# Rotary embedding with cached tables: one VectorE operation for both products of a chunk, from interleaved tables

## The chip, the cores and the metric

One core of one Trainium2 chip. The metric is the device time of one execution in microseconds (us), lower is better; each kernel was run several times beside the kernel before on the same chip.

## The reference, cut to what matters

```python
def setup_inputs():
    batch, n_heads, seq, head_dim = (8, 8, 1024, 64)
    ...
    return {'x': np.random.randn(batch, n_heads, seq, head_dim).astype(np.float32), 'cos_cached': ..., 'sin_cached': ...}

def reference(x, cos_cached, sin_cached):
    half = x.shape[-1] // 2
    x_first, x_second = (x[:, :, :, :half].copy(), x[:, :, :, half:].copy())
    out_first = x_first * cos_cached - x_second * sin_cached
    out_second = x_first * sin_cached + x_second * cos_cached
    return np.concatenate([out_first, out_second], axis=-1).astype(np.float32)
```

16.8 MB of x are read and 16.8 MB written, all fp32. Per element there are two products and one sum.

## The kernel before

x is cut into 8 units of 2 MB: 128 partitions, each with 64 rows of 64 elements. A unit is loaded into its own tile, rotated in place and stored from there. Most units go in three chunks (24, 24 and 16 rows) like this: ScalarE copies ("stages") a chunk into PSUM; VectorE multiplies the staged rows by the sine table into a separate tile `s` and by the cosine table into x; and then somebody makes the sums: POOL (GpSimd), VectorE itself (the chunks called "alone"), or TensorE, which adds by multiplying with plus and minus the identity and whose result ScalarE copies back. Unit 2 is worked on by POOL from end to end.

```python
def products(pt, u, n0, n1, alone=False):
    xr, sr, pr = rows(xt[u], n0, n1), rows(s_of(u), n0, n1), rows(pt, 0, n1 - n0)
    mul(nc.vector, sr, pr, tab(sn, n0, n1))
    mul(nc.vector, pr if alone else xr, pr, tab(cs, n0, n1))
    if alone:
        sums(nc.vector, xr, pr, sr)
...
on_pool(2, 0, 32)                       # unit 2: products and sums on POOL, two halves
cuts = ((0, 24), (24, 48), (48, 64))
chunks = [(u, n0, n1) for u in (1, 3, 4, 5, 6, 7) for n0, n1 in cuts]
alone = {(1, 48), (3, 48), (6, 48), (7, 24), (7, 48)}
...
for c, (u, n0, n1) in enumerate(chunks):
    products(st[c], u, n0, n1, (u, n0) in alone)
    put(c + 2)                          # ScalarE stages the chunk after next
    if c in back:
        pe_back(*back[c])               # ScalarE copies a TensorE sum tile back into x
    if c in on_pe:
        pe_sums(*on_pe[c])
    for f, *args in behind.get(c, ()):  # POOL's sums, and the stores
        f(*args)
```

All loads of x and all stores are issued on one queue, that of the sync engine, in the order: sine table, units 0 to 7; then stores of units 0, 1, 3, 2, 4, 5, 6 and of unit 7 in two pieces, "7a" (48 rows) and "7b" (16 rows).

## Time and profile before

| | before |
|---|---|
| time, median | 85.84 us (3 runs, 85.73 to 85.88) |
| span in the profile | 83.8 us |
| VectorE busy | 72.3 us (86%) |
| POOL busy | 65.9 us (79%) |
| DMA, share of 16 engines' span | 96% |
| last store issued / landed | 77.3 / 82.7 us |

"Landed" is the issue time plus the profile's time from issue to landing. The lines themselves stand in the prediction below.

### The profile page before, as it was taken

The numbers are of one execution on the slowest core, as the hardware profiler recorded it, in microseconds if no ns is written. First come the engines' busy times: TensorE is split into PE (matmuls) and PEld (weight loads), VectorE is DVE, ScalarE is ACT, GpSimd is POOL, SyncE is SP. The second block draws the span as 40 slices with busy tenths as digits, with TensorE's granted clock in tenths as the row PEclk, the third lists the DMA queues.
The fourth block names the chain that finished last, engine by engine and source line by source line (L and its number), as shares of the span: only waits on it lengthen the run. The fifth ranks groups of instructions, "written<-read, shape, count | busy, mean of one in ns | idle before, by whom it ended". The sixth has DMA issues, their size and how long they took to land. (4 is left out here: it accounts for less than half of the span.)

```text
span 83.8 us, 409 instructions
## 1 busy us (share of the span) xinstructions
PE 42.4 (51%) x80; PEld 16.2 (19%) x80; DVE 72.3 (86%) x56; ACT 37.2 (44%) x32; POOL 65.9 (79%) x35
## 2 busy tenths in 40 slices
PE   0299910003994965949469089594959800000000
PEld 0234100002341403314033042231404200000000
DVE  1284999999999999999999999999999999998000
ACT  4100694464066553674636951976346852000000
POOL 5059959999999999999999999999999959400000
PEclk9999999999999999999999999999999999655555
DMA  2999999999999999999999999999999999999990
GB/s 59 309 411 450 415 461 391 461 415 454 415 415 454 399 469 399 446 422 415 352 415 446 415 446 407 462 415 446 422 422 454 399 450 407 462 415 434 417 385 23
DMA packets 2689, 33.83 MB, mean 404 GB/s; under 512 B 320, under 2 KB 320, under 8 KB 512
## 3 DMA queue, kind: packets, MB, share of 16 engines
q1 hardware_dynamic: 2640, 33.69, 95.7%
q10 hardware_dynamic: 48, 0.13, 0.4%
q14 instruction: 1, 0.01, 0.0%
HBM read 17.04 MB, written 16.78 MB: 404 GB/s over the span
## 5 line engine op out<-in xcount | busy, mean ns | idle before, releaser
L97 ACT COPY st<-x 128x1536 f32<-128x1536 f32 (+1 forms) x18 | 23.4, 1302 | 18.2 <-DVE x L83 10.2
L161 PE MATMUL acc<-x,ones 128*128 128x512 f32 x36 | 20.4, 650 | 20.6 <-ACT x L167 11.3
L83 DVE TENSOR_TENSOR s<-st,sn 128x1536 f32<-128x1536 f32 (+1 forms) x18 | 28.2, 1568 | 0.0
L83 DVE TENSOR_TENSOR x<-st,cs 128x1536 f32<-128x1536 f32 (+1 forms) x13 | 21.6, 1663 | 0.0
L86 POOL TENSOR_TENSOR x<-x,s 128x1024 f32<-128x1024 f32 (+3 forms) x7 | 15.8, 2262 | 1.9 <-ACT x L167 0.9
L87 POOL TENSOR_TENSOR x<-x,s 128x1024 f32<-128x1024 f32 (+3 forms) x7 | 15.8, 2258 | 0.0
L161 PEld LDWEIGHTS acc<-x,ones 128*128 128x128 f32 x36 | 6.6, 204 | 33.6 <-ACT x L167 17.9
L167 ACT COPY x<-acc 128x1024 f32<-128x1024 f32 x9 | 9.1, 1010 | 6.5 <-PE acc L162 6.5
L162 PE MATMUL acc<-s,minus 128*128 128x512 f32 x18 | 10.1, 644 | 0.0
L83 POOL TENSOR_TENSOR x<-x,cs 128x2048 f32<-128x2048 f32 x2 | 9.1, 4540 | 0.2
L162 PE MATMUL acc<-s,ones 128*128 128x512 f32 x18 | 9.2, 592 | 0.0
L83 POOL TENSOR_TENSOR g<-x,sn 128x2048 f32<-128x2048 f32 x2 | 9.1, 4532 | 0.0
L83 DVE TENSOR_TENSOR st<-st,cs 128x1024 f32<-128x1024 f32 (+1 forms) x5 | 6.6, 1328 | 0.0
L139 POOL COPY sn<-sn 32x1024 f32<-32x1024 f32 x3 | 3.1, 1032 | 3.4 <-DVE sn L136 3.3
L133 PE MATMUL en<-raw,ones 32*128 32x512 f32 x4 | 3.7, 1089 | 3.7 <-DMA raw<-in_sin_cached_dram 3.7
L86 POOL TENSOR_TENSOR x<-x,g 128x1024 f32<-128x1024 f32 x2 | 4.7, 2350 | 0.2
L97 ACT COPY pre<-x 128x2048 f32<-128x2048 f32 x1 | 1.9, 1870 | 6.6 <-DMA x<-in_x_dram 6.6
L87 POOL TENSOR_TENSOR x<-x,g 128x1024 f32<-128x1024 f32 x2 | 4.7, 2358 | 0.0
L162 PEld LDWEIGHTS acc<-s,minus 128*128 128x128 f32 x18 | 3.7, 206 | 4.9 <-issue 4.9
L162 PEld LDWEIGHTS acc<-s,ones 128*128 128x128 f32 x18 | 3.4, 190 | 4.3 <-issue 4.3
L86 DVE TENSOR_TENSOR x<-st,s 128x512 f32<-128x512 f32 (+1 forms) x5 | 3.7, 745 | 0.2
L87 DVE TENSOR_TENSOR x<-st,s 128x512 f32<-128x512 f32 (+1 forms) x5 | 3.7, 733 | 0.0
(23 smaller groups left out, 25.9 us busy)
## 6 DMA issues: line engine op xcount, KB each, us to landing
x<-in_x_dram SPq DMA_DIRECT2D x7, 2048.0 KB, 24.8
out_dram<-x SPq DMA_DIRECT2D x7, 2048.0 KB, 10.1
x<-in_x_dram SPq DMA_DIRECT2D x2, 1024.0 KB, 6.4
out_dram<-x SPq DMA_DIRECT2D x1, 1536.0 KB, 7.7
out_dram<-x SPq DMA_DIRECT2D x1, 512.0 KB, 5.4
raw<-in_cos_cached_dram ACTq DMA_DIRECT2D x1, 128.0 KB, 3.2
raw<-in_sin_cached_dram SPq DMA_DIRECT2D x1, 128.0 KB, 2.8
```

Source lines behind the costliest of these rows:

```text
L83: eng.tensor_tensor(out=o, in0=a, in1=t, op=TT.mult)
L86: eng.tensor_tensor(out=o[:, :, 0], in0=c[:, :, 0], in1=s[:, :, 1], op=TT.subtract)
L87: eng.tensor_tensor(out=o[:, :, 1], in0=c[:, :, 1], in1=s[:, :, 0], op=TT.add)
L97: nc.scalar.copy(out=pt[:, :(n1 - n0) * hd], in_=xt[u][:, n0 * hd:n1 * hd])
L133: nc.tensor.matmul(part, sel, r, start=True, stop=True)
L139: nc.gpsimd.tensor_copy(out=t[k * Q:(k + 1) * Q, C:], in_=t[0:Q, C:])
L161: nc.tensor.matmul(a[:, k], plus, xr[:, :, k], start=True, stop=False)
L162: nc.tensor.matmul(a[:, k], plus if k else minus, sr[:, :, 1 - k], start=False, stop=True)
L167: nc.scalar.copy(out=rows(xt[u], n0, n0 + G), in_=a)
```

## The change

The aim was to relieve VectorE of operations, and POOL of part of unit 2. The two tables are interleaved in one tile (32 cosines, 32 sines per row), and each unit's tile lies beside a "room" for sine products, shared with a second unit, so that one VectorE operation can write both products: its output steps from the room to the unit (a step of one whole unit, or of 40 rows for unit 7, backwards for some) and its input reads the staged rows twice. The time won pays for the products of 24 rows of unit 2, which POOL no longer makes. Two chunks lose their "alone" sums, one TensorE sum tile goes, POOL takes those sums, and the negated identity is made by ScalarE.

```diff
-    cs = const.tile([P, T], fp32, name="cs")
-    sn = const.tile([P, T], fp32, name="sn")
+    tb = const.tile([P, 2 * T], fp32, name="tb")
+    tb4 = tb.rearrange("p (n t j) -> p n t j", t=2, j=half)
 ...
+    for i, (u0, u1) in enumerate(((3, 6), (0, 4), (1, 5))):
+        w = xp.tile([P, 3 * F], fp32, name=f"w{i}")
+        xt[u0], xt[u1] = w[:, :F], w[:, 2 * F:]
+        sv[u0] = sv[u1] = w[:, F:2 * F]
+        px[u0], px[u1] = both(w[:, :2 * F]), both(w[:, F:])[:, :, ::-1]
+    K = 40
 ...
-    nc.vector.tensor_scalar_mul(out=minus, in0=plus, scalar1=-1.0)
+    nc.scalar.mul(out=minus, in_=plus, mul=-1.0)
 ...
-        mul(nc.vector, sr, pr, tab(sn, n0, n1))
-        mul(nc.vector, pr if alone else xr, pr, tab(cs, n0, n1))
+        if u not in px:                 # rows of unit 2: two operations as before
+            ...
+        xr = pt[:, :n * hd].rearrange("p (n o f) -> p n o f", o=1, f=hd)
+        tr = tb4[:, n0:n1].unsqueeze(3).to_broadcast([P, n, 2, 2, half])
+        mul(nc.vector, px[u][:, n0:n1].rearrange("p n t (k j) -> p n t k j", k=2),
+            xr.to_broadcast([P, n, 2, hd]).rearrange("p n t (k j) -> p n t k j", k=2), tr)
 ...
-    on_pool(2, 0, 32)
+    on_pool(2, 0, K // 2)
 ...
+    chunks.insert(9, (2, K, R))
-    alone = {(1, 48), (3, 48), (6, 48), (7, 24), (7, 48)}
+    whole = {(6, 48), (7, 24), (7, 48)}
 ...
-        1: [(pool_sums, 1, 32, 48), (on_pool, 2, 32, 64)],
-        3: [(store, 1)],
-        8: [(store, 3), (store, 2), (pool_sums, 4, 16, 64)],
-        9: [(store, 4)],
+        2: [(pool_sums, 1, 16, 64), (store, 1)],
+        5: [(pool_sums, 3, 32, 64), (on_pool, 2, K // 2, K)],
+        6: [(store, 3)],
+        9: [(pool_sums, 2, K, 64), (store, 2), (pool_sums, 4, 32, 64), (store, 4)],
```

More of the change, by code (lines that the diff above doesn't have):

```diff
@@ L42 @@
     xp = ctx.enter_context(tc.tile_pool(name="xp", bufs=1))
-    tv = ctx.enter_context(tc.tile_pool(name="tv", bufs=3))
-    tg = ctx.enter_context(tc.tile_pool(name="tg", bufs=1))
-    cs = const.tile([P, T], fp32, name="cs")
-    sn = const.tile([P, T], fp32, name="sn")
+    tb = const.tile([P, 2 * T], fp32, name="tb")
+    tb4 = tb.rearrange("p (n t j) -> p n t j", t=2, j=half)
     ones = const.tile([P, 2 * P], fp32, name="ones")
@@ L50, with both @@
     minus = const.tile([P, P], fp32, name="minus")
-    raw = tv.tile([P, F], fp32, name="raw", tag="s")
-    rs, rc = raw[0:Q, 0:C], raw[0:Q, C:2 * C]
+    xt, sv, px = {}, {}, {}
+    def both(t):
+        return t.rearrange("p (w n f) -> p n w f", w=2, f=hd)
+    for i, (u0, u1) in enumerate(((3, 6), (0, 4), (1, 5))):
[4 more added lines that the diff above has]
+    K = 40
+    w = xp.tile([P, K * hd + F], fp32, name="w3")
+    gt, xt[7] = w[:, :K * hd], w[:, K * hd:]
+    sv[7], px[7] = gt, both(w[:, :2 * K * hd])[:, :, ::-1]
+    xt[2], sv[2] = xp.tile([P, F], fp32, name="x2"), sv[3]
+    rs, rc = sv[3][0:Q, 0:C], sv[3][0:Q, C:2 * C]
     nc.sync.dma_start(out=rs, in_=sin_cached.rearrange("(q n) j -> q (n j)", q=Q))
     nc.scalar.dma_start(out=rc, in_=cos_cached.rearrange("(q n) j -> q (n j)", q=Q))
-    xt = [xp.tile([P, F], fp32, name=f"x{u}") for u in range(n_u)]
     for m0, m1 in ((0, F // 2), (F // 2, F)):
@@ L72 @@
                             base=0, pattern=[[-1, P]], channel_multiplier=1)
-    nc.vector.tensor_scalar_mul(out=minus, in0=plus, scalar1=-1.0)
+    nc.scalar.mul(out=minus, in_=plus, mul=-1.0)
+    cs, sn = tb4[:, :, 0], tb4[:, :, 1]
     def rows(t, n0, n1):
@@ L78, in tab, with flat @@
     def tab(t, n0, n1):
-        v = t[:, n0 * half:n1 * half].rearrange("p (n o j) -> p n o j", o=1, j=half)
-        return v.to_broadcast([P, n1 - n0, 2, half])
+        return t[:, n0:n1].unsqueeze(2).to_broadcast([P, n1 - n0, 2, half])
+    def flat(t):
+        return t.rearrange("p (n j) -> p n j", j=half)
     def mul(eng, o, a, t):
@@ L87, in sums, with products, alone @@
         eng.tensor_tensor(out=o[:, :, 1], in0=c[:, :, 1], in1=s[:, :, 0], op=TT.add)
-    sv = {}
-    def s_of(u):
-        if u not in sv:
-            sv[u] = tv.tile([P, F], fp32, name="s", tag="s")
-        return sv[u]
     def stage(pt, u, n0, n1):
         nc.scalar.copy(out=pt[:, :(n1 - n0) * hd], in_=xt[u][:, n0 * hd:n1 * hd])
-    def products(pt, u, n0, n1, alone=False):
-        xr, sr, pr = rows(xt[u], n0, n1), rows(s_of(u), n0, n1), rows(pt, 0, n1 - n0)
+    def products(pt, u, n0, n1):
+        n = n1 - n0
+        if u not in px:
+            for o, t in ((sv[u], sn), (xt[u], cs)):
+                mul(nc.vector, rows(o, n0, n1), rows(pt, 0, n), tab(t, n0, n1))
+            return
+        xr = pt[:, :n * hd].rearrange("p (n o f) -> p n o f", o=1, f=hd)
+        tr = tb4[:, n0:n1].unsqueeze(3).to_broadcast([P, n, 2, 2, half])
+        mul(nc.vector, px[u][:, n0:n1].rearrange("p n t (k j) -> p n t k j", k=2),
+            xr.to_broadcast([P, n, 2, hd]).rearrange("p n t (k j) -> p n t k j", k=2), tr)
+    def alone(pt, u, n0, n1):
+        s = sv[4] if u == 7 else sv[u]
+        xr, sr, pr = rows(xt[u], n0, n1), rows(s, n0, n1), rows(pt, 0, n1 - n0)
         mul(nc.vector, sr, pr, tab(sn, n0, n1))
-        mul(nc.vector, pr if alone else xr, pr, tab(cs, n0, n1))
-        if alone:
-            sums(nc.vector, xr, pr, sr)
+        mul(nc.vector, pr, pr, tab(cs, n0, n1))
+        sums(nc.vector, xr, pr, sr)
     def on_pool(u, n0, n1):
-        g = tg.tile([P, F // 2], fp32, name="g")
-        xr, gr = rows(xt[u], n0, n1), rows(g, 0, n1 - n0)
+        xr, gr = rows(xt[u], n0, n1), rows(gt, n0, n1)
         mul(nc.gpsimd, gr, xr, tab(sn, n0, n1))
@@ L115, in pool_sums @@
         xr = rows(xt[u], n0, n1)
-        sums(nc.gpsimd, xr, xr, rows(s_of(u), n0, n1))
+        sums(nc.gpsimd, xr, xr, rows(sv[u], n0, n1))
     def store(u, n0=0, n1=R):
@@ L135 @@
         for t, r in ((sn, rs), (cs, rc)):
-            nc.vector.stream_shuffle(t[0:Q, C:], r, odd)
-        for t in (sn, cs):
-            for k in range(1, P // Q):
-                nc.gpsimd.tensor_copy(out=t[k * Q:(k + 1) * Q, C:], in_=t[0:Q, C:])
-        mul(nc.vector, rows(s_of(0), 0, H), rows(xt[0], 0, H), tab(en, 0, H))
+            nc.vector.stream_shuffle(t[0:Q, H:], flat(r), odd)
+        for k in range(1, P // Q):
+            nc.gpsimd.tensor_copy(out=tb4[k * Q:(k + 1) * Q, H:], in_=tb4[0:Q, H:])
+        mul(nc.vector, rows(sv[0], 0, H), rows(xt[0], 0, H), tab(flat(en), 0, H))
         for i in range(2):
             xr = rows(xt[0], i * G, (i + 1) * G)
-            mul(nc.vector, xr, xr, tab(ec[i], 0, G))
+            mul(nc.vector, xr, xr, tab(flat(ec[i]), 0, G))
         pool_sums(0, 0, H)
         stage(pre, 0, H, R)
-        nc.scalar.copy(out=sn[:, :C], in_=en)
+        nc.scalar.copy(out=sn[:, :H], in_=flat(en))
         for i in range(2):
-            nc.scalar.copy(out=cs[:, i * BK:(i + 1) * BK], in_=ec[i])
+            nc.scalar.copy(out=cs[:, i * G:(i + 1) * G], in_=flat(ec[i]))
         products(pre, 0, H, R)
@@ L158, in pe_sums @@
         a = acc[u, n0].rearrange("p (k n j) -> p k n j", k=2, j=half)
-        xr, sr = rows(xt[u], n0, n0 + G), rows(s_of(u), n0, n0 + G)
+        xr, sr = rows(xt[u], n0, n0 + G), rows(sv[u], n0, n0 + G)
         for k in range(2):
@@ L167, in pe_back @@
         nc.scalar.copy(out=rows(xt[u], n0, n0 + G), in_=a)
-    on_pool(2, 0, 32)
+    on_pool(2, 0, K // 2)
     cuts = ((0, 24), (24, 48), (48, 64))
     chunks = [(u, n0, n1) for u in (1, 3, 4, 5, 6, 7) for n0, n1 in cuts]
-    alone = {(1, 48), (3, 48), (6, 48), (7, 24), (7, 48)}
-    on_pe = {0: (1, 0), 1: (1, 16), 3: (3, 0), 4: (3, 16), 6: (3, 32), 8: (4, 0),
-             9: (5, 0), 11: (5, 16), 12: (6, 0)}
-    back = {1: (1, 0), 3: (1, 16), 4: (3, 0), 6: (3, 16), 8: (3, 32), 9: (4, 0),
-            11: (5, 0), 12: (5, 16), 14: (6, 0)}
-    behind = {
-        1: [(pool_sums, 1, 32, 48), (on_pool, 2, 32, 64)],
-        3: [(store, 1)],
-        8: [(store, 3), (store, 2), (pool_sums, 4, 16, 64)],
-        9: [(store, 4)],
-        11: [(pool_sums, 5, 32, 64)],
-        12: [(store, 5)],
-        13: [(pool_sums, 6, 16, 48)],
-        14: [(store, 6)],
-        15: [(pool_sums, 7, 0, 24)],
-        16: [(store, 7, 0, 48)],
-        17: [(store, 7, 48, 64)],
+    chunks.insert(9, (2, K, R))
+    whole = {(6, 48), (7, 24), (7, 48)}
+    on_pe = {0: (1, 0), 3: (3, 0), 4: (3, 16), 6: (4, 0), 7: (4, 16), 10: (5, 0),
+             11: (5, 16), 13: (6, 0)}
+    back = {2: (1, 0), 4: (3, 0), 6: (3, 16), 8: (4, 0), 9: (4, 16), 11: (5, 0),
+            13: (5, 16), 15: (6, 0)}
+    behind = {
+        2: [(pool_sums, 1, 16, 64), (store, 1)],
+        5: [(pool_sums, 3, 32, 64), (on_pool, 2, K // 2, K)],
+        6: [(store, 3)],
+        9: [(pool_sums, 2, K, 64), (store, 2), (pool_sums, 4, 32, 64), (store, 4)],
+        12: [(pool_sums, 5, 32, 64)],
+        13: [(store, 5)],
+        14: [(pool_sums, 6, 16, 48)],
+        15: [(store, 6)],
+        16: [(pool_sums, 7, 0, 24)],
+        17: [(store, 7, 0, 48)],
+        18: [(store, 7, 48, 64)],
     }
@@ L202 @@
     for c, (u, n0, n1) in enumerate(chunks):
-        products(st[c], u, n0, n1, (u, n0) in alone)
+        (alone if (u, n0) in whole else products)(st[c], u, n0, n1)
         put(c + 2)
```

## The prediction

> **What bounds the kernel now.** I read the page's activity rows first, because one of them decides the case: which row is full in every slice.
>
> ```profile
> DVE  1284999999999999999999999999999999998000
> POOL 5059959999999999999999999999999959400000
> DMA  2999999999999999999999999999999999999990
> GB/s 59 309 411 450 415 461 391 461 415 454 415 415 454 399 469 399 446 422 415 352 415 446 415 446 407 462 415 446 422 422 454 399 450 407 462 415 434 417 385 23
> ...
> q1 hardware_dynamic: 2640, 33.69, 95.7%
> ...
> HBM read 17.04 MB, written 16.78 MB: 404 GB/s over the span
> ```
>
> VectorE and POOL are full from 10 to about 70 us, but DMA is full from the second slice to the last but one, and its one queue is busy 95.7% of the span. The view by windows says whether "full" means moving bytes at one rate, or waiting:
>
> ```profile
> 28.00:44.00 16.00, 11.45 (x27) 4.42 (x26) 15.97 (x13) 8.36 (x9) 15.84 (x7) 1.00 1.00 417
> 44.00:60.00 16.00, 11.48 (x27) 4.45 (x26) 16.00 (x12) 10.52 (x9) 15.92 (x6) 1.00 1.01 432
> 60.00:78.00 18.00, 5.56 (x13) 1.99 (x11) 17.21 (x15) 5.80 (x5) 11.27 (x6) 0.83 1.00 429
> ```
>
> The last two columns are the DMA share and GB/s: the share is 1.00 and the rate 417 to 432 in each, loads (to 44 us) and stores (after it) alike. Then the stores: first their issues in the sync queue's timeline, then, in the same order, their times to landing in the DMA view, each asked for alone (units 3 and 2, and the two last pieces of unit 7, called 7a and 7b):
>
> ```profile
> 48.53 0.33 SPq L119 DMA_DIRECT2D out_dram<-x  x1
> ...
> 51.75 0.33 SPq L119 DMA_DIRECT2D out_dram<-x  x1
> ...
> 73.79 0.33 SPq L119 DMA_DIRECT2D out_dram<-x  x1
> ...
> 77.34 0.33 SPq L119 DMA_DIRECT2D out_dram<-x  x1
> ```
>
> ```profile
> out_dram<-x SPq DMA_DIRECT2D x1, 2048.0 KB, 9.7
> ...
> out_dram<-x SPq DMA_DIRECT2D x1, 2048.0 KB, 11.4
> ...
> out_dram<-x SPq DMA_DIRECT2D x1, 1536.0 KB, 7.7
> ...
> out_dram<-x SPq DMA_DIRECT2D x1, 512.0 KB, 5.4
> ```
>
> Issue plus landing time gives when each ends. The last load (x7) is issued at 6.55 and lands 37.1 later, at 43.65; the stores in issue order (units 0, 1, 3, 2, 4, 5, 6, 7a, 7b) land at 48.6, 53.4, 58.2, 63.15, 68.0, 73.05, 77.9, 81.5 and 82.7. The steps of the 2 MB ones are 4.8 to 5.0 us, with no longer one among them: **no store ever came late.** Each was issued while the one ahead of it was still moving. The chain of waits shows VectorE (38% of the span) up to the last store's issue at 77.34, which looks as if VectorE set the end. It does not: 7b waited in the queue behind 7a until about 81. The queue sets the end, and it moves the same bytes before and after.
>
> **Slack.** In the windows, the first packets move at about 1.7 us, 1.0 after the first issue at 0.74; at the end the packets stop at about 82.2, some 0.5 before the last landing. So a store leaves no gap if it is issued by (landing of the one ahead) - 0.5 - 1.0. Latest harmless issues: unit 2 at 56.7, unit 4 at 61.65, 5 at 66.5, 6 at 71.55, 7a at 76.4, 7b at 80.0. Before, they were issued at 51.75, 58.53, 63.15, 67.78, 73.79 and 77.34: 2.6 to 5 us early.
>
> **What the Trainium skill says.** "VectorE: DVE Perf Modes", § The perf-mode tier table: fp32 tensor_tensor, and any with a PSUM operand, runs at 1x, one element a cycle; § The TRN2 errata gives an fp32 add of N elements as (N+151)/0.96 ns. The trace agrees: 1757 by that for N = 1536 against 1746 measured, 691 for 512 against 692. So merging two products halves neither reads nor time; it saves a fixed part. "SBUF — State Buffer", § Who interferes with whom: a VectorE instruction with at most one SBUF input does not contend with GpSimd. The trace fits: POOL's 1024-element sums keep 2.34 us beside a VectorE that never rests, and the merged operation again has one input in PSUM (the staged rows) and one in SBUF (the table). "DMA: Bandwidth & Descriptors", § Where 436 GB/s comes from: a ceiling of 435 GB/s on the SBUF side; the windows' 429 to 432 lie 1% below, so no change to the engines can make the transfers much quicker.
>
> **The change part by part.** Prices, from the groups by form and two rows of the timeline:
>
> ```profile
> L83 DVE TENSOR_TENSOR s<-st,sn 128x1536 f32<-128x1536 f32 x12 | 21.0, 1746 | 0.0
> L86 DVE TENSOR_TENSOR x<-st,s 128x512 f32<-128x512 f32 x4 | 2.8, 692 | 0.1
> L86 POOL TENSOR_TENSOR x<-x,s 128x1024 f32<-128x1024 f32 x4 | 9.4, 2340 | 0.9 <-POOL cs L139 0.9
> L83 POOL TENSOR_TENSOR g<-x,sn 128x2048 f32<-128x2048 f32 x2 | 9.1, 4532 | 0.0
> ```
>
> ```profile
> 16.52 1.75 DVE L83 TENSOR_TENSOR s<-st,sn 128x1536 f32<-128x1536 f32 x1
> 18.19 1.75 DVE L83 TENSOR_TENSOR x<-st,cs 128x1536 f32<-128x1536 f32 x1
> ```
>
> The starts are 1.67 apart: 1.60 for 1536 elements at 0.96 a ns, and 0.07 fixed. The sums walk all three operands in runs of 32 and still fit the same line, so I take the new patterns (runs of 64, a step to the room beside the unit and back) to cost nothing either. A merged operation on 24 rows is then 3072/0.96 = 3.20 + 0.07 = 3.27 from start to start, and on 16 rows 2.20.
>
> VectorE, by starts: 16 merged pairs (unit 0's second half, eleven of 24 rows, four of 16) save 16 x 0.07 = 1.1. Two chunks (units 1 and 3, last 16 rows) no longer make their own sums: four at 0.61, 2.4. The negated identity moves to ScalarE: 0.15. Added: 24 rows of unit 2, two products, 3.3. One wait gets longer: a merged operation needs both tables, and POOL's copies now start only when both shuffles are done (6.05), three of 2048 at about 2.06, so they end at 12.4, where VectorE went on at 12.12: 0.3. Sum: -1.1 - 2.4 - 0.15 + 3.3 + 0.3, about 0. Going through the order: unit 0 to 16.8; unit 1 (3.27 + 3.27 + 2.20 = 8.73) to 25.5; unit 3 to 34.3; unit 4 to 43.0; the rows of unit 2 to 46.3; unit 5 to 55.1; unit 6 (two merged, then products and sums of 16 rows as before, 3.6) to 65.2, where unit 7 began at 65.12 before. Then 3.27, 5.2 and 3.7 as before: 7a ready at 73.7, 7b at 77.3. **The last store is issued within 0.3 us of where it was.** VectorE's busy time (full durations) falls by 0.23 for the identity, 2.7 for sums and 16 x 0.146 = 2.3, and rises by 3.5: 72.3 to about 70.5, in 37 instructions for 56.
>
> POOL (sums 0.165 us + 2.125 per thousand elements of one operand, from 1252 at 512 and 2340 at 1024; products about 2.97 for 20 rows by starts): unit 0's sums from 12.5, four of 2.3, to 21.7; 20 rows of unit 2 (2 x 2.97 + 3.03) to 30.6; unit 1's 48 rows of sums, 6.8, to 37.4 (store 1 at 37.5, before 37.87); unit 3's 32 rows, 4.6, to 42.0 (store 3 at about 42.1, six earlier, and worth nothing: the queue takes it at about 53); the other 20 rows of unit 2 to 51.0; sums of the 24 rows VectorE multiplied, 3.55, to 54.55; units 4, 5 and 6 at 4.6 each to 59.15, 63.75, 68.35. All inputs are there well before, by the VectorE times. So store 2 goes out at 54.6 (2.85 later than before), 4 at 59.2, 5 at 63.8, 6 at 68.4. Slack left: 2.1, 2.45, 2.7 and 3.1 us, then 2.7 for 7a and 2.7 for 7b. POOL's busy time stays near 66.6.
>
> TensorE and ScalarE each lose one of nine 16-row sum tiles; neither is full. On the sync queue: the same transfers in the same order, every store in time. Sum for the end: **0**.
>
> **Rivals.** (1) The merged operation is slower than one element a cycle, because it jumps 16 KB between writes or re-reads PSUM. Against it: the strided sums fit the plain line. The merged pairs hold 4096 + 11 x 3072 + 4 x 2048 elements, 48 us; 5% dearer costs 2.4 us, which the slack of 7b just swallows; 10% (4.8) puts 2.1 us into the end, about 88. (2) POOL becomes the bound for store 2: it has almost no rest from 12.5 to 54.6, and 42 us of work against 2.1 of slack allows 5%. POOL 10% slower by contention would add 2.1 us too, about 87.9. For it: POOL's spans are rough, and the slack is more than halved here; against it, the one-SBUF-input rule holds as before. (3) It gets faster, if VectorE set the end: then freeing VectorE would pull in the last store and the end with it. Against it: 7b already waits 4 us in the queue; issued any earlier it lands at the same time. At best the rate rises by the 1% left, 0.8 us, and nothing here touches the rate.
>
> **Range and chances.** The time is 85.84 with a spread of 0.15; I take 85.85. Slack of 2 us guards both main rivals, so the range is mostly noise with a tail upward: 85.5 to 86.5. A gain of 2% would need 1.7 us out of a stream already at 99% of the quoted ceiling: 0.01. A loss of 2% needs 1.7 us of gap, thus VectorE's merged operations or POOL some 9% dearer than their prices, or an unseen wait: 0.05. The rest, 0.94, is the same.
>
> **What would show it right or wrong.** Right: the DMA row again full, its share 1.00 from 12 to 78 us; stores landing in steps of 4.8 to 5.0; a mean near 3346 ns for the merged 24-row operation; store 2 issued near 54.6 with about 8.5 us to landing in place of 11.4; 7b issued near 77.3. Wrong: a step between landings over 5.2 us, a dip in the DMA row after 44 us, a merged operation over 3500 ns, POOL's sums over 2.4 us at 1024 elements, or VectorE waiting for POOL at a shared sine room.

## The result, and the profile after

| | before | after |
|---|---|---|
| time, median | 85.78 us (6 runs, 85.73 to 85.88) | 85.99 us (6 runs, 85.91 to 86.28) |
| ratio, 95% interval | | 1.0028 (1.0012 to 1.0043) |
| span of the profiled run | 83.8 us | 83.5 us |
| VectorE busy, instructions | 72.3 us, 56 | 71.7 us, 37 |
| POOL busy | 65.9 us | 65.9 us |
| last store issued / landed | 77.3 / 82.7 us | 77.1 / 82.4 us |

By the 2% rule the two are the same; the 0.3% is clear of the noise and is looked at below.

The page of the changed kernel, its activity rows and its queue:

```profile
DVE  0293999999999999999999999999999999999000
POOL 5009989999999999999999999999999999400000
DMA  2999999899998989989999999999999999999990
GB/s 29 285 432 479 408 392 487 377 495 385 424 455 377 502 377 440 440 377 502 369 424 447 400 455 408 463 416 432 440 424 424 416 463 416 447 424 420 430 385 37
...
q1 hardware_dynamic: 2640, 33.69, 95.9%
```

The DMA row is as full as before (95.9% for 95.7%; the few eights all lie before 38 us). Two windows of the changed kernel (last columns: DMA share, GB/s):

```profile
44.00:60.00 16.00, 11.10 (x24) 4.31 (x24) 16.00 (x7) 10.17 (x10) 15.84 (x9) 1.00 1.00 430
60.00:78.00 18.00, 3.70 (x8) 1.44 (x8) 17.01 (x14) 5.04 (x5) 11.96 (x6) 0.73 1.00 429
```

The rates are within 2 GB/s of before's 432 and 429. The stores of units 3 and 2 and the two pieces of unit 7, first as the sync queue's timeline has their issues, then as the DMA view has size and time to landing:

```profile
42.12 0.33 SPq L143 DMA_DIRECT2D out_dram<-w  x1
...
54.62 0.33 SPq L143 DMA_DIRECT2D out_dram<-x  x1
...
73.59 0.33 SPq L143 DMA_DIRECT2D out_dram<-w  x1
...
77.14 0.33 SPq L143 DMA_DIRECT2D out_dram<-w  x1
```

```profile
out_dram<-w SPq DMA_DIRECT2D x1, 2048.0 KB, 15.9
...
out_dram<-x SPq DMA_DIRECT2D x1, 2048.0 KB, 8.3
...
out_dram<-w SPq DMA_DIRECT2D x1, 1536.0 KB, 7.6
...
out_dram<-w SPq DMA_DIRECT2D x1, 512.0 KB, 5.3
```

Store 3 is issued 6.4 us earlier than before and only waits longer in the queue (15.9 us for 9.7): it lands at 58.0, before at 58.2. Store 2 is issued 2.9 us later and waits less (8.3 for 11.4): it lands at 62.9, before at 63.15. The whole set of landings, 48.4, 53.2, 58.0, 62.9, 67.75, 72.7, 77.5, 81.2 and 82.4, has steps of 4.8 to 4.9 us for 2 MB. What moved on the engines is absorbed by the queue. The groups by form:

```profile
L104 DVE TENSOR_TENSOR w<-st,tb 128x3072 f32<-128x3072 f32 x11 | 36.4, 3346 | 0.0
L107 POOL TENSOR_TENSOR w<-w 128x1024 f32<-128x1024 f32 x6 | 14.1, 2347 | 0.4 <-POOL tb L162 0.4
L104 POOL TENSOR_TENSOR w<-x,tb 128x1280 f32<-128x1280 f32 x2 | 5.8, 2903 | 0.0
```

One merged operation on 24 rows takes 3346 ns; two single ones took 1746 each, 3492 together. The merge saves only a small fixed part and no work per element. POOL's sums kept their price (2347 for 2340).

### The profile page after: what moved, and what is told of

The parts are those of the page before. It is cut to its first block, busy times and chain, and to the rows that moved or that the text cites. A ratio compares the mean times of both kernels' runs of the same rounds, so it can differ in the third digit from the quotient of the medians.

```text
span 83.5 us, 372 instructions
## 1 busy us (share of the span) xinstructions
PE 38.6 (46%) x72; PEld 14.8 (18%) x72; DVE 71.7 (86%) x37; ACT 37.6 (45%) x33; POOL 65.9 (79%) x36
## 3 DMA queue, kind: packets, MB, share of 16 engines
q1 hardware_dynamic: 2640, 33.69, 95.9%
## 5 line engine op out<-in xcount | busy, mean ns | idle before, releaser
L104 DVE TENSOR_TENSOR w<-st,tb 128x3072 f32<-128x3072 f32 (+3 forms) x19 | 50.6, 2728 | 0.0
L111 ACT COPY st<-w 128x1536 f32<-128x1536 f32 (+1 forms) x18 | 23.4, 1302 | 21.6 <-DVE w L104 14.8
L184 PE MATMUL acc<-w,ones 128*128 128x512 f32 x32 | 18.2, 652 | 21.5 <-ACT w L190 12.4
L107 POOL TENSOR_TENSOR w<-w 128x1024 f32<-128x1024 f32 (+2 forms) x8 | 19.3, 2414 | 0.4 <-POOL tb L162 0.4
L108 POOL TENSOR_TENSOR w<-w 128x1024 f32<-128x1024 f32 (+2 forms) x8 | 19.3, 2410 | 0.0
L184 PEld LDWEIGHTS acc<-w,ones 128*128 128x128 f32 x32 | 5.9, 205 | 33.2 <-ACT w L190 18.2
L162 POOL COPY tb<-tb 32x2048 f32<-32x2048 f32 x3 | 5.7, 1885 | 4.7 <-DVE tb L160 4.7
L185 PE MATMUL acc<-w,minus 128*128 128x512 f32 x16 | 9.1, 650 | 0.0
L190 ACT COPY w<-acc 128x1024 f32<-128x1024 f32 x8 | 8.1, 1007 | 1.3 <-PE acc L185 1.3
L185 PE MATMUL acc<-w,ones 128*128 128x512 f32 x16 | 8.2, 592 | 0.0
L104 POOL TENSOR_TENSOR x<-x,tb 128x1280 f32<-128x1280 f32 x2 | 5.8, 2906 | 0.2
L104 POOL TENSOR_TENSOR w<-x,tb 128x1280 f32<-128x1280 f32 x2 | 5.8, 2903 | 0.0
L107 POOL TENSOR_TENSOR x<-x,w 128x640 f32<-128x640 f32 (+1 forms) x3 | 4.9, 1628 | 0.2
L108 POOL TENSOR_TENSOR x<-x,w 128x640 f32<-128x640 f32 (+1 forms) x3 | 4.9, 1637 | 0.0
L185 PEld LDWEIGHTS acc<-w,ones 128*128 128x128 f32 x16 | 3.0, 190 | 3.8 <-issue 3.8
```

The costliest lines, as they stand in the source:

```text
L104: eng.tensor_tensor(out=o, in0=a, in1=t, op=TT.mult)
L107: eng.tensor_tensor(out=o[:, :, 0], in0=c[:, :, 0], in1=s[:, :, 1], op=TT.subtract)
L108: eng.tensor_tensor(out=o[:, :, 1], in0=c[:, :, 1], in1=s[:, :, 0], op=TT.add)
L111: nc.scalar.copy(out=pt[:, :(n1 - n0) * hd], in_=xt[u][:, n0 * hd:n1 * hd])
L162: nc.gpsimd.tensor_copy(out=tb4[k * Q:(k + 1) * Q, H:], in_=tb4[0:Q, H:])
L184: nc.tensor.matmul(a[:, k], plus, xr[:, :, k], start=True, stop=False)
```

## The experiments

Theory A: the DMA queue sets the end, and the engines have a stated slack (2 to 3 us) in front of it. Rival B: VectorE's end sets the time, and the change is neutral because the 24 rows eat what the merging won. Both give the same time for the change, so only doses and cuts can tell them apart.

For each dose, the harmless latest issue of a store is the landing of the one ahead minus 1.5 us (the prediction's rule), here from the changed kernel's landings: store 2 at 56.5, store 7a at 76.0, store 7b at 79.7.

**1. The merge undone** (each merged operation split again; all else as changed).

```diff
-        if u not in px:
+        if True:
```

> The changed kernel with each merged operation split again into its two products (16 pairs), all else kept. Theory A (the DMA queue sets the end; engine work has about 2.6 us to spare): VectorE about 16 x 0.07 = 1.1 us longer, last store issued near 78.2 in place of 77.1, time unchanged: 86.0, within 0.3. Rival B (VectorE's end sets the time): 1.1 us longer, about 87.1.

Measured: 86.14 us (6 runs), ratio to before 1.0038 (1.0011 to 1.0065). The last store was issued at 78.05, 0.9 us later than with the merge. The 16 saved fixed parts exist, nearly as priced, and the end hardly feels them: the spans average 83.8 us for 83.55 with the merge, 0.3 longer where B wanted 1.1.

**2. The 24 rows left out** (wrong result; the transfers stay).

```diff
-        (alone if (u, n0) in whole else products)(st[c], u, n0, n1)
+        if (u, n0) not in skip:         # skip = {(2, 40)}
+            (alone if (u, n0) in whole else products)(st[c], u, n0, n1)
 ...
-        9: [(pool_sums, 2, K, 64), (store, 2), ...
+        9: [(store, 2), ...
```

> Wrong result on purpose: the 24 rows of unit 2 that the change gave to VectorE are stored unrotated, so that VectorE has 3.3 us and POOL 3.6 us less to do; all transfers stay. A: time unchanged, 86.0 within 0.3; last store issued near 73.8 and landing at about 82.4 as before. B: 3.3 us shorter, about 82.7.

Measured: 85.80 us, ratio to before 0.9993 (0.9967 to 1.0020). The last store was issued at 75.46, not at 73.8: VectorE gained only 1.7 us, as it then stood 1.6 us at unit 5's first chunk (44.4). Still, 1.7 us less on VectorE and 3.7 us less ahead of store 2 (issued at 50.94) bought nothing: the spans of its runs average 83.6 us, those of the changed kernel 83.55. (The span runs from the first recorded instruction to the last; the time outside it differs between these programs by up to 0.6 us, see run 10, so small differences are read from spans.) B is wrong.

**3. and 4. More work on VectorE**, in front of the last two stores: one sine product of 24 rows made twice, and the merged operation of unit 7 made three times. Both repeat a computation that gives the same numbers, so the results are right.

```diff
 (3)
-        mul(nc.vector, sr, pr, tab(sn, n0, n1))
+        for _ in range(2 if (u, n0) == (7, 24) else 1):
+            mul(nc.vector, sr, pr, tab(sn, n0, n1))
 (4)
         (alone if (u, n0) in whole else products)(st[c], u, n0, n1)
+        for _ in range(2 if (u, n0) == (7, 0) else 0):
+            products(st[c], u, n0, n1)
```

> The changed kernel with one product of unit 7 (24 rows, sine) made twice: VectorE 1.67 us longer ahead of the last two stores. A: 7a issued near 75.3 (harmless until 76.0), 7b near 78.8 (harmless until 79.7): time unchanged, 86.0 within 0.3. B: 1.7 longer, 87.7.

> The changed kernel with the merged operation on unit 7's first 24 rows made three times in place of once: VectorE 2 x 3.27 = 6.5 us longer. A: 7a issued at 80.1 against 76.0, so the queue stands idle for about 4.1 us and the time is 90.1. B: 6.5 longer, 92.5.

Measured: with 1.7 us more, 85.57 us, ratio 0.9959 (0.9932 to 0.9987): no loss (span 83.65 for 83.55), with 7a issued at 75.31 and 7b at 78.86, 0.7 and 0.8 us inside the harmless limits. With 6.5 us more, 89.82 us, ratio 1.0460 (1.0434 to 1.0486): 3.8 us over the changed kernel against 4.1 expected by A and 6.5 by B. Store 7a went out at 80.42, 4.4 late, and the span grew by 4.3 (87.9 for 83.55, means); the time outside the span was 0.55 us shorter, and that makes it 3.8. The sync queue's issue of 7a and the page's rate row of that run show the hole:

```profile
80.42 0.33 SPq L143 DMA_DIRECT2D out_dram<-w  x1
```

```profile
GB/s 30 317 421 425 477 365 470 425 410 477 358 477 418 418 477 358 477 395 440 462 373 477 403 433 470 365 477 425 410 462 395 455 455 380 358 0 39 408 405 103
```

One slice of 2.2 us with 0 and one with 39 GB/s, right where 7a is missing: the first hole in the stream of stores, and the span grows by about its length.

**5. and 6. More work on POOL** ahead of store 2: one extra product of 10 rows (1.6 us), and two extra products of 20 rows (5.9 us).

```diff
 (5)
         sums(nc.gpsimd, xr, xr, gr)
+        if n0:
+            mul(nc.gpsimd, rows(gt, 0, 10), rows(gt, 0, 10), tab(sn, 0, 10))
 (6)
-        mul(nc.gpsimd, gr, xr, tab(sn, n0, n1))
+        for _ in range(3 if n0 else 1):
+            mul(nc.gpsimd, gr, xr, tab(sn, n0, n1))
```

> The changed kernel with one more product of 10 rows on POOL ahead of store 2: POOL 1.6 us longer. A: store 2 issued at 56.2 against 56.5 harmless: time unchanged, 86.0 within 0.3; a POOL that set the end would add 1.6.

> The changed kernel with the sine product of POOL's second 20 rows of unit 2 made three times: POOL 2 x 2.97 = 5.9 us longer ahead of store 2. A: store 2 issued at 60.5 against 56.5 harmless, so 4.0 us of idle queue, 90.0. B: only VectorE's wait for the shared sine room counts (unit 6 waits for the sums of unit 2's rows), about 2.2 us, 88.2.

Measured: with 1.6 us more, 85.73 us (5 runs), ratio 0.9984 (0.9972 to 0.9996). Store 2 was issued at 56.37 against 56.44 harmless (store 3 landed at 57.94 there): the slack is used up to the last 0.1 us and neither the time nor the span (83.5) has moved. With 5.9 us more, 90.08 us, ratio 1.0488 (1.0469 to 1.0507): 4.1 us over the changed kernel for 4.0 expected by A and 2.2 by B. Store 2 went out at 60.61, 4.1 late, and the span grew by 4.2. The rate row has its hole after store 3:

```profile
GB/s 30 325 418 422 471 403 441 471 366 471 381 463 433 403 471 366 478 403 411 403 441 433 418 448 418 433 15 0 478 411 426 471 366 478 359 478 392 415 409 99
```

**7. The stream started earlier**: the sine table moved to ScalarE's queue, so that x is first on the sync queue. This was meant to beat both kernels.

```diff
-    nc.sync.dma_start(out=rs, in_=sin_cached....)
+    nc.scalar.dma_start(out=rs, in_=sin_cached....)
     nc.scalar.dma_start(out=rc, in_=cos_cached....)
```

> The changed kernel with the sine table's load moved from the sync queue to ScalarE's queue, ahead of the cosine's, so that x is the first thing on the sync queue. A: the stream starts 0.4 to 0.5 us earlier and ends so: 85.5 to 85.6; tables may land up to 1 us later, which the slack of 2.6 us hides. B: VectorE starts no earlier, time the same or up to 1 us longer.

Measured: 87.55 us, ratio to before 1.0199 (1.0173 to 1.0225): 1.6 us slower than the changed kernel; the expectation failed. The tables were not "up to 1 us" later. VectorE's timeline of this run:

```profile
5.07 1.27 DVE L160 STREAM_SHUFFLE tb<-w 32x1024 f32<-32x1024 f32 x1
8.77 0.01 DVE L160 LOAD_MASK_SELECT tb<-w  x1 [2.42 <-DMA w<-in_cos_cached_dram]
```

VectorE took the cosines at 8.77, as they landed, where it had taken them at 4.93 without this edit: 3.8 us later. POOL's table copies start behind them (10.19 for 6.36), and POOL carries the delay to store 2, issued at 58.04 for 54.62. The stream was late as well: from 1.75 to 9.75 us the DMA engines moved 323 GB/s, in the changed kernel 393, and store 3 landed at 59.05, 1.05 us after the changed kernel's, so store 2's limit was 57.55 and it missed it by 0.5. Together 1.55 us, the measured loss (1.55 in the spans too). The Trainium skill, "DMA: Bandwidth & Descriptors", § Issuing engines are not separate DMA queues, says that transfers of two queues share the same 16 engines and interleave; the run agrees, and shows the price for the small one: 7.6 us to landing for 128 KB, issued at 1.17.

**8. and 9. One store less** (wrong result: unit 0 is never stored), in both kernels, each tried twice: if the queue has 4.85 us less to do, does the change then help?

```diff
-    store(0)
```

> Wrong result on purpose: the changed kernel without the store of unit 0, so that the queue has one 2 MB transfer (4.85 us) less. A: the queue now runs dry once, before store 2 (issued 54.6, needed by about 51.7), so it gains only 4.85 - 2.9 = 1.95 us: about 84.0. B (VectorE sets the end): no gain, 86.0.

> Wrong result on purpose: the kernel before without the store of unit 0. A: the queue runs dry before store 3 (issued 48.5, needed by 47.1) by 1.4 us and before store 4 by 0.3, so it gains 4.85 - 1.7 = 3.1 us: about 82.7, so 1.2 us ahead of the changed kernel with the same store left out: the change ate slack, which shows only when the queue has less to do. B: no gain, 85.8, level with the changed kernel.

Measured at first: changed kernel 84.33 us (84.25 to 84.47, ratio to the whole kernel before 0.9820), near the 84.0 expected. Kernel before 84.98 us, but over a wide range (83.79 to 85.17, of which the last counts as slow), against 82.7 expected. The profiled run, at 85.0, has a wait that the profile of the full kernel does not show. TensorE's timeline in it, with the granted clock at 0.59 from 50 to 54 us in the windows:

```profile
49.71 1.76 PE L162 MATMUL acc<-s,minus 128*128 128x512 f32 x2
51.27 1.91 PE L161 MATMUL acc<-x,ones 128*128 128x512 f32 x2
```

Pairs of matmuls that take 1.02 elsewhere take 1.76 and 1.91. ScalarE waits 3.5 us for that sum tile, and the staging copy for unit 6 stands behind it in ScalarE's order; VectorE then waits for the staged rows:

```profile
54.18 1.01 ACT L167 COPY x<-acc 128x1024 f32<-128x1024 f32 x1 [3.53 <-PE acc L162]
55.09 2.82 ACT L97 COPY st<-x 128x1536 f32<-128x1536 f32 x2
```

```profile
56.57 1.76 DVE L83 TENSOR_TENSOR s<-st,sn 128x1536 f32<-128x1536 f32 x1 [1.43 <-ACT st L97]
```

If this is why the gain stayed out, runs should fall into two groups. Both kernels were run again side by side:

> The kernel before without unit 0's store, once more. In its first run a fall of the granted TensorE clock at 49 to 53 us made one sum tile late, ScalarE's staging stood behind that tile's copy and VectorE waited 1.4 us. If that is the cause of the missing gain, runs fall in two groups, about 83.5 without such a wait and 85.0 with it; if something else is, all lie near 85.0.

> The changed kernel without unit 0's store, once more beside the above: 84.3 as in its first run, in one group, since store 2's issue time (POOL) sets it and no engine waits for TensorE.

Measured: kernel before 83.79, 83.86, 83.87 and, apart from these, 84.96, 85.08, 85.14 us (two of the latter count as slow, over 1.5% above the fastest); changed kernel 84.17 to 84.54, one group. The profile of a run of the lower group (83.79) shows the same tile at full speed and no wait of VectorE there:

```profile
49.70 1.02 PE L162 MATMUL acc<-s,minus 128*128 128x512 f32 x2
50.56 1.02 PE L161 MATMUL acc<-x,ones 128*128 128x512 f32 x2
```

So the two groups are there, and the two profiles differ by the clock at this tile. For the other runs of the groups there is no such look; their mean clock does not tell them apart (0.918 to 0.925 in the upper group, 0.914 to 0.939 in the lower). The Trainium skill, "TensorE: Matmul & The Clock Gate", § Part 1: The HAM clock gate, says that TensorE's clock drops to half after an idle window of about 3.4 us. The slow profile agrees in the size (granted clock 0.50 from 50 to 52 us) but not in the trigger: TensorE had stood idle for only 2.3 us (until 48.74), and in the full kernel's profile it idles 2.3 us at the same place and keeps its clock. Why one execution has it there and another not, no run here shows.

Taking undisturbed runs, the kernel before took 83.84 us and the changed one 84.26. Nearly all of these 0.4 us lie outside the recorded span (2.07 for 2.47, see run 10): the spans average 81.77 and 81.84. So the 1.2 us that A expected between the two did not show. The store left out gained the changed kernel 1.7 us of span for 1.95 expected, which refutes B's "no gain", but the kernel before only 2.0 for 3.1. In the latter's profile at 83.79 the queue stood still for 2.0 us before store 3 instead of 1.4, since store 1 landed at 48.2, 0.4 earlier than I had set, and store 3 was issued 0.2 later. A further half microsecond is seen from 74 to 76 us, where the DMA share falls to 0.72, just after the issue of 7a at 73.98. By the rule 7a was 0.3 in time (store 6 landed at 75.78), so the rule is not exact there; why, stays open.

**10. The changed kernel again**, for the 0.3%.

> The changed kernel once more, unaltered. If its 0.3% over the kernel before is its own, then again about 86.0, with some 2.45 us of it outside the recorded span (2.05 for the kernel before) and a span 0.2 us shorter than before's; if it was the job's, then level with before, 85.8.

Measured: 86.07 us, ratio 1.0022 (1.0008 to 1.0036). The difference is the kernel's own. In that job its span averages 83.52 us and the kernel before's 83.76, so inside the recorded span it is 0.24 us shorter; the time outside the span averages 2.50 us for 2.06, 0.44 longer. The sum is the 0.2 us. That outer part is not tied to the change's idea: with one more POOL product (run 5) it averages 2.19, with more VectorE work (3 and 4) 1.91 and 1.93, and these kernels differ from the changed one by one or two instructions. What happens there the trace does not show, and it stays open. It also makes most of run 3's lead over the kernel before, in spite of its added work: 0.15 us less outside, 0.1 inside. Of all these kernels none is clearly ahead of the one before for a reason that could be built on.

## Why the prediction was right

- **The bound.** Said: the queue, full from 1.7 to 82.2 us. Shown: removing work from VectorE and POOL (2) gained nothing beyond noise, adding up to the slack (3, 5) cost nothing, and exceeding it (4, 6) cost the excess: stores 4.4 and 4.1 late, spans 4.3 and 4.2 longer. VectorE as the bound (the third rival, B here) is refuted by all of these.
- **The slack rule** (landing of the one ahead minus 1.5 us). It held to 0.1 us in 5 and gave 7's loss after the fact; in the kernel before without unit 0's store it missed by about half a microsecond. It is what the forecast of no loss rested on.
- **The issue times.** Said: store 2 at 54.6, 4 at 59.2, 5 at 63.8, 6 at 68.4, 7a at 73.7, 7b at 77.3. Measured: 54.62, 59.25, 63.87, 68.48, 73.59, 77.14. Prices by start-to-start from one trace carried to another order within 0.2 us.
- **The merged operation.** Said: 3346 ns. Measured: 3346. The first rival (a dearer pattern) did not come about, nor the second (contention on POOL).
- **Busy times, slightly off.** VectorE 71.7 for 70.5: the term that failed is "16 x 0.146 = 2.3". The busy row counts a moment once, and successive operations overlap by 0.08 us in the trace, so a removed operation in a row takes only its start-to-start part, 0.07, out of it: 72.3 - 0.23 (the identity, which stood alone) - 2.4 - 1.1 + 3.3 = 71.9. POOL 65.9 for 66.6: three table copies of 2048 took 1885 ns where I had 2060. They ended at 12.10, so the 0.3 us that VectorE was to wait for them did not occur (it went on at 12.29 without a pause).
- **The time.** Said: 85.85 in 85.5 to 86.5. Measured: 85.99. Stream and engines account for none of the 0.2 us; it lies outside the span.

## What to carry to other kernels

Before crediting a cheaper operation, look for the resource without a gap: here the landings of the stores came at even steps, and each store had been issued 2 us or more before its turn. Then the useful number for a change is not how much busy time it saves but how it moves the issue time of each transfer against the latest harmless one; inside that slack neither gain nor loss reaches the time, and beyond it the excess does (here to within about half a microsecond). Merging two fp32 tensor products on VectorE saves one fixed part of about 0.07 us, not a pass over the data.

## What the Trainium skill lacked or had wrong

- "DMA: Bandwidth & Descriptors", § Where 436 GB/s comes from, says that between HBM and SBUF the HBM side (about 358) binds. Here a core alone moved 417 to 428 GB/s while it loaded (12 to 44 us) and 429 to 432 while it stored. "HBM Reference", § Specifications (TRN2), has it right (about 425 for a core streaming alone).
- "DMA: Bandwidth & Descriptors", § Specifications, gives about 0.6 us to the first byte on this path without saying from when. The runs show 1.0 us from the start of the first issue (0.74) to the first packets (1.75), and 0.6 from its end (1.13). For a store from the sync queue it has no time from issue to landing; here a 2 MB one on an idle queue took 6.3 us.
- The same page, § Issuing engines are not separate DMA queues, has no figure for a small transfer beside large ones: 128 KB took 7.6 us to land as the second on ScalarE's queue with 1 MB and 2 MB loads on the other, against 3.3 alone on it.
- "VectorE: DVE Perf Modes", § The TRN2 errata, does not say whether an input in PSUM read twice and an output with a far or backward step keep (N+151)/0.96. Here they do: 3357 ns by that for N = 3072, measured 3346.
- No page says why the time outside the recorded span varies between nearly equal programs, here from 1.9 to 2.6 us; it would belong to "Runtime: NRT & Kernel Launch".
